# A third k pair in seven block products in the gate and up projections of a decoder trunk on one Trainium2 core

## The chip, the cores and the metric

The kernel runs on one core of a Trainium2 chip. The metric is the device time of one execution in microseconds, taken as the median of several runs. TensorE (PE) multiplies, VectorE (DVE) and ScalarE (ACT) prepare its operands, GpSimd (POOL) does little, and SyncE (SP) issues the weight loads.

## The reference: what is computed

Two decoder layers run over one sequence of 256 rows of width 2048, in float32. Layer 0 mixes by sliding-window attention and an mLSTM, layer 1 by forgetting attention. Every layer then has a SwiGLU feed-forward part of hidden width 5632, and a final RMS norm ends the trunk:

```python
def swiglu(xn, w_gate, w_up, w_down):
    return (jax.nn.silu(xn @ w_gate) * (xn @ w_up)) @ w_down
...
        h = h + mix.astype(h.dtype)
        h = h + swiglu(rms_norm(h, norm_ffn[layer]), w_gate[layer], w_up[layer], w_down[layer])
```

## The kernel before

**Three products for one.** Every large product is made of float32r operands. A tile is split into a rounded part `hi` (an ACT copy) and a rest `lo` (a DVE subtraction), and x·w becomes x_hi·w_hi + x_hi·w_lo + x_lo·w_hi: three matmuls of 128x128 against 128x512 (`three`, L344; `gemm`, L150). The activations are kept transposed and split in `xh`, `xl` (16 k tiles of 128, each with two row tiles t = 0, 1).

**Loads.** `load_raw` (L85) brings 256 rows of k by 512 columns (512 KB) on SP's queue into `raw`, which has four buffers. `split_chunk` (L138) makes `hi` and `lo` of it; these have four buffers each. So the raws of two k pairs are in the core at a time (one chunk of gate and one of up for each), and the splits of two.

**Gate and up.** `gate_up` (L352) makes one block of 512 hidden columns, for both row tiles, gate and up: four sums of 128x512. There are eleven blocks a layer, six and five with a down projection behind each group (`HALVES`), so 22 blocks in all. A block goes through eight k pairs in the order of this list, whose entries are (kind, pair):

```python
ORDER = ((0, 0), (0, 1), (1, 2), (0, 4), (0, 5), (1, 3), (0, 6), (0, 7))
MIXED = [p for w, p in ORDER if w]
```

A *plain* pair (kind 0, L359 to L370) splits one gate and one up chunk and makes 2 matrices x 2 k tiles x 2 row tiles x 3 = 24 matmuls into the four `plain` banks. A *mixed* pair (kind 1, L371 to L402) sees the same work as a 2x2 by 2x2 block product (rows: the two row tiles; inner: the two k tiles; columns: gate and up) and makes it of seven block products in place of eight, by sums of blocks: 7 x 3 = 21 matmuls. Four of the seven go into four banks of their own (`mixed`), three into `plain`. Its operands take more work: four differences of weight blocks (`t4`, L378 to L381), their splits `ht`, `lt` in two halves (L386 to L391, two buffers each; L240 and L241 within `split_plain`), the split of the gate chunk (L376), and that of half of the up chunk (L384). The sums of activations are made once a layer: `sums_of` (L199) fills one slot of `sh`, `sl` for each mixed pair, called from `split_scaled` (L213) while the output projection (`out_proj`, L332) delivers the layer's input, 512 columns (two k pairs) at a time.

**The end of a block.** The four mixed banks are folded into `c` (an ACT copy, L405, and four DVE additions, L406 to L409), then the four plain banks are added (L413), then come SiLU (L428), the product (L430), eight transposes (L438) and a split into the down projection's operands (L440 to L443).

**Banks.** PSUM has two pools of four banks. A block's plain banks lie in one pool and its mixed banks in the other, and the next block swaps them (`par`, L425). So the next block's plain sums start in the banks from which L405 to L409 have read, and its mixed products in those that L413 and the transposes have left.

**What sets the order.** The loops above give dependences and a priority; the framework's scheduler then fixes one order of instructions for each engine at build time, and PE's order interleaves neighbouring pairs and blocks. On the chip every engine goes through its own list in order and waits on semaphores.

Of the kernel before, what the change touches and what calls it, by code (L numbers as in the profile page):

```python
# [30 lines left out]
OFF_QM, OFF_KM, OFF_VM, OFF_OM = 1536, 2048, 2560, 3584  # L31
CAP = 15.0
FILL = 24
ORDER = ((0, 0), (0, 1), (1, 2), (0, 4), (0, 5), (1, 3), (0, 6), (0, 7))
MIXED = [p for w, p in ORDER if w]
HALVES = (0, 6, 11)

# [2 lines left out]
def trunk(  # L40
# [311 lines left out]
    def gate_up(fp, sh, sl, layer, g, par):  # L352
        c0 = g * NB
        plain = [[bank(par, "acc") for _ in range(NT)] for _ in range(2)]
        mixed = None
        count = [s_[0] for s_ in ORDER]
        for pos, (w, pair) in enumerate(ORDER):
            k0 = 2 * pair
            if not w:  # L359
                for m, wt in enumerate((w_gate[layer], w_up[layer])):  # L360
                    hi, lo = load_chunk(wt, k0, c0, NB)
                    for i in range(CK):
                        ah, al = x_of(k0 + i)
                        for t in range(NT):
                            ts = slice(t * P, (t + 1) * P)
                            three(
                                plain[m][t], ah[:, ts], al[:, ts], hi[:, i, :], lo[:, i, :],
                                pos == 0 and i == 0, pos == len(ORDER) - 1 and i == CK - 1,
                            )
# [518 lines left out]
```

## Time and profile before

| | |
|---|---|
| median of 3 runs | 2187.59 us (2187.58 to 2188.13) |
| the profiled execution | 2186.29 us, of it the profile's span 2184.6 us |
| granted TensorE clock, mean | 0.998 |
| busy: PE, DVE, ACT, POOL | 99%, 66%, 49%, 2% |
| HBM traffic | 186 GB/s over the span |
| matmuls of lines 345 to 347 (gate and up) | 3 x 1364 |

A row of the costliest groups gives busy time in total and the mean duration of one instruction; because an engine starts the next instruction before the last one is through, the spacing of starts in the timeline can be shorter than that duration. A timeline row gives the start in us, the duration in us, engine, line, operation, tiles, and in brackets the idle time before it with what ended it. Rows of SPq are the issues of loads.

In the text a pair is named by its kind and its place in the block's order: P0, P1, M2, P3, P4, M5, P6, P7 before. "Gate" and "up" are its two chunks.

### The profile page before, as it was taken

To read this page: it belongs to the slowest core of one execution; us is meant where nothing else is said; L and a number is where in the kernel's file an instruction comes from. 1 tells how busy PE (TensorE), PEld (TensorE's weight loads), DVE (VectorE), ACT (ScalarE), POOL (GpSimd) and SP (SyncE) were. 2 spreads that over 40 slices of the span, in tenths; PEclk is the share of its full clock that TensorE was granted. 3 is DMA by queue.
4 is the path that set the end of the run, shared out by engine and by line. 5 is a ranking of instruction groups with operands and counts; after the bars stand their busy time and mean duration, and the time that the engine had idled before them with its cause. 6 is when DMAs were issued, how large, how long until landed. Compare 5 with 4: busy or idle time off the path is not lost.

```text
span 2184.6 us, 26574 instructions
## 1 busy us (share of the span) xinstructions
PE 2164.8 (99%) x10052; PEld 1796.9 (82%) x10052; DVE 1442.0 (66%) x1732; ACT 1078.5 (49%) x1397; POOL 38.4 (2%) x61
## 2 busy tenths in 40 slices
PE   8999999999999999999999999999999999999998
PEld 6878888888888888888888888888888888888886
DVE  5565566788754677865555555668778645777754
ACT  5565455555543455544545544555455434554543
POOL 2110000000000000000010000000000000000000
PEclk9999999999999999999999999999999999999999
DMA  8544556666666666566675565566666665666664
GB/s 258 150 147 148 171 167 184 203 186 208 187 194 193 201 192 195 190 196 190 176 229 167 164 178 157 177 184 195 208 184 197 198 193 183 208 192 199 194 191 144
DMA packets 213536, 408.33 MB, mean 187 GB/s; under 512 B 12736, under 2 KB 21024, under 8 KB 213152
## 3 DMA queue, kind: packets, MB, share of 16 engines
q1 hardware_dynamic: 212736, 402.90, 60.0%
q0 software_dynamic: 624, 3.72, 0.5%
q8 instruction: 78, 1.28, 0.2%
q14 instruction: 50, 0.41, 0.1%
q10 hardware_dynamic: 48, 0.02, 0.0%
HBM read 404.48 MB, written 2.11 MB: 186 GB/s over the span
## 4 chain that ended last, share of the span: by engine, by line
PE 98%; ACT 1%; DMA 1%; issue 0%; DVE 0%; SPq 0%; POOLq 0%; POOL 0%; ACTq 0%
PE acc L164 17%; PE acc L165 17%; PE acc L166 17%; PE acc L346 12%; PE acc L347 12%; PE acc L345 12%; PE prod L346 2%; PE prod L345 2%; PE prod L347 2%; PE pf L438 1%; DMA h<-in_x_dram 1%; PE p L269 1%; PE ptm L252 1%; PE pt L219 1%; PE po L320 1%; PE pp L312 0%
## 5 line engine op out<-in xcount | busy, mean ns | idle before, releaser
L142 DVE TENSOR_TENSOR lo<-raw,hi 128x1024 fp32r<-128x1024 f32 (+3 forms) x732 | 876.7, 1206 | 597.0 <-ACT hi L141 595.7
L141 ACT CAST hi<-raw 128x1024 fp32r<-128x1024 f32 (+3 forms) x732 | 752.3, 1034 | 825.3 <-PE acc L166 515.1
L347 PE MATMUL acc<-hi,xl 128*128 128x512 f32 x1100 | 429.7, 391 | 0.0
L346 PE MATMUL acc<-lo,xh 128*128 128x512 f32 x1100 | 428.5, 390 | 0.0
L345 PE MATMUL acc<-hi,xh 128*128 128x512 f32 x1100 | 423.8, 391 | 0.0
L164 PE MATMUL acc<-hi,mh 128*128 128x512 f32 x768 | 300.6, 392 | 1.2 <-ACT mh L240 1.2
L165 PE MATMUL acc<-lo,mh 128*128 128x512 f32 x768 | 300.7, 392 | 0.0
L166 PE MATMUL acc<-hi,ml 128*128 128x512 f32 x768 | 298.3, 390 | 0.0
L165 PE MATMUL acc<-lo,xh 128*128 128x512 f32 (+3 forms) x736 | 276.3, 376 | 0.4 <-DVE lo L142 0.4
L164 PE MATMUL acc<-hi,xh 128*128 128x512 f32 (+3 forms) x736 | 275.2, 378 | 1.2 <-ACT hi L141 1.2
L166 PE MATMUL acc<-hi,xl 128*128 128x512 f32 (+3 forms) x736 | 276.2, 376 | 0.0
L347 PEld LDWEIGHTS acc<-hi,xl 128*128 128x128 f32 x1100 | 206.5, 188 | 42.5
L346 PEld LDWEIGHTS acc<-lo,xh 128*128 128x128 f32 x1100 | 206.6, 188 | 42.4
L345 PEld LDWEIGHTS acc<-hi,xh 128*128 128x128 f32 x1100 | 206.6, 188 | 41.9
L164 PEld LDWEIGHTS acc<-hi,mh 128*128 128x128 f32 x768 | 144.2, 188 | 31.0 <-ACT mh L240 1.4
L166 PEld LDWEIGHTS acc<-hi,ml 128*128 128x128 f32 x768 | 144.2, 188 | 29.7
L165 PEld LDWEIGHTS acc<-lo,mh 128*128 128x128 f32 x768 | 144.2, 188 | 29.4
L240 ACT CAST ht<-t 128x1024 fp32r<-128x1024 f32 x88 | 92.6, 1052 | 138.9 <-DVE t L379 113.6
L164 PEld LDWEIGHTS acc<-hi,xh 128*128 128x128 f32 x736 | 138.4, 189 | 26.5 <-issue 2.0
L165 PEld LDWEIGHTS acc<-lo,xh 128*128 128x128 f32 x736 | 139.1, 189 | 24.6 <-DVE lo L142 1.1
L166 PEld LDWEIGHTS acc<-hi,xl 128*128 128x128 f32 x736 | 139.1, 189 | 24.1 <-issue 0.3
L241 DVE TENSOR_TENSOR lt<-t,ht 128x1024 fp32r<-128x1024 f32 x88 | 107.2, 1218 | 0.0
(273 smaller groups left out, 1897.5 us busy)
## 6 DMA issues: line engine op xcount, KB each, us to landing
raw<-in_w_gate_dram SPq DMA_DIRECT2D x176, 512.0 KB, 4.0
raw<-in_w_up_dram SPq DMA_DIRECT2D x176, 512.0 KB, 4.5
raw<-in_w_down_dram SPq DMA_DIRECT2D x176, 512.0 KB, 3.7
raw<-in_w_in_odd_dram SPq DMA_DIRECT2D x88, 512.0 KB, 3.8
raw<-in_w_in_even_dram SPq DMA_DIRECT2D x64, 512.0 KB, 3.9
raw<-in_w_out_even_dram SPq DMA_DIRECT2D x32, 512.0 KB, 3.7
raw<-in_w_out_odd_dram SPq DMA_DIRECT2D x32, 512.0 KB, 3.7
raw<-in_w_in_odd_dram SPq DMA_DIRECT2D x8, 272.0 KB, 2.8
```

Source lines behind the costliest of these rows:

```text
L141: nc.scalar.copy(hi[:, :, 0:n], raw[:, :, 0:n])
L142: nc.vector.tensor_tensor(out=lo[:, :, 0:n], in0=raw[:, :, 0:n], in1=hi[:, :, 0:n].bitcast(F32), op=ALU.subtract)
L164: nc.tensor.matmul(o, ah[:, ts], hi, start=(k == 0), stop=False)
L165: nc.tensor.matmul(o, ah[:, ts], lo, start=False, stop=False)
L166: nc.tensor.matmul(o, al[:, ts], hi, start=False, stop=(k == k_all - 1))
L219: nc.tensor.transpose(pt[:, i, t, :], h[:, t, k * P : (k + 1) * P], ident)
L240: nc.scalar.copy(dst_h, src)
L241: nc.vector.tensor_tensor(out=dst_l, in0=src, in1=dst_h.bitcast(F32), op=ALU.subtract)
L252: nc.tensor.transpose(pt[:, i, :], s_, ident)
L345: nc.tensor.matmul(o, ah, hi, start=start, stop=False)
L346: nc.tensor.matmul(o, ah, lo, start=False, stop=False)
L347: nc.tensor.matmul(o, al, hi, start=False, stop=stop)
```

## The change

The order list gets a third mixed entry (pair 1), and the pairs are set out so that mixed ones stand at places 2, 4 and 6 with a plain one between:

```diff
-ORDER = ((0, 0), (0, 1), (1, 2), (0, 4), (0, 5), (1, 3), (0, 6), (0, 7))
+ORDER = ((0, 0), (0, 4), (1, 1), (0, 5), (1, 2), (0, 6), (1, 3), (0, 7))
 MIXED = [p for w, p in ORDER if w]
```

In the names above the order is then P0, P1, M2, P3, M4, P5, M6, P7. `sh` and `sl` grow by a slot (from 2 to 3), `sums_of` is called three times a layer in place of twice, and the place-1 pair of a block is k pair 4 where it was k pair 1. The number and size of the loads are the same.

## The prediction

> **What bounds the kernel now.** I read the page's busy times first, then what PE waits for, then one block of gate and up in the middle of the first group (449.87 to 493.00 us), as a window and instruction by instruction.
>
> ```profile
> PE 2164.8 (99%) x10052; PEld 1796.9 (82%) x10052; DVE 1442.0 (66%) x1732; ACT 1078.5 (49%) x1397; POOL 38.4 (2%) x61
> ```
>
> ```profile
> PE acc L164 <- ACT hi L141: 1.2, 2, 0.7
> PE acc L164 <- ACT mh L240: 1.2, 1, 1.2
> PE acc L165 <- DVE lo L142: 0.4, 2, 0.2
> ```
>
> Apart from the start, these are all the waits of PE that the view of waits lists (us, times, longest): none is at lines 345 to 347. In the blocks PE never waits. The window (busy us by engine, clock, DMA share, GB/s) says what room the others have:
>
> ```profile
> 449.87:493.00 43.13, 43.13 (x196) 35.69 (x195) 34.80 (x41) 22.25 (x25) 0.00 (x0) 1.00 0.64 195
> ```
>
> PE is busy all 43.13 us at clock 1.00, DVE 34.80, ACT 22.25. DVE is the next to bind, with 8.3 us to spare. PE's own pace is in its timeline, which runs through M5 (467.37 to 472.13) and P6 (to 477.57):
>
> ```profile
> 467.37 0.39 PE L345 MATMUL prod<-hi,xh 128*128 128x512 f32 x1
> ...
> 472.13 0.39 PE L345 MATMUL acc<-hi,xh 128*128 128x512 f32 x1
> ...
> 477.57 0.39 PE L345 MATMUL acc<-hi,xh 128*128 128x512 f32 x1
> ```
>
> 21 matmuls in 4.76 us and 24 in 5.44 are both 0.2267 us each. The 0.39 us of a row is latency, not pace: priced by it, a matmul would look 1.7 times too dear. A block is 186 matmuls (6 x 24 + 2 x 21), 42.16 us, and about 0.96 for its eight transposes.
>
> **What is removed.** One plain pair becomes mixed: 24 - 21 = 3 matmuls, 3 x 0.2267 = 0.68 us a block, 15.0 us over 22 blocks. A block would take 42.44 us. PE is the bound, so this is gained in full unless something else comes to be late.
>
> The Trainium skill (TensorE: Matmul & The Clock Gate, Back-to-back issue gap) gives 216 ns for an isolated gap at N=512 and a sustained 131 ns with weight loads between; the 66 matmuls would by these estimates be worth 14.3 or 8.6 us. The trace shows 0.2267 us with a weight load before each, so the measured pace decides.
>
> **What DVE gets.** Its timeline around M5's preparation, the folding of the mixed banks, and M2 of the next block:
>
> ```profile
> 458.42 0.69 DVE L378 TENSOR_TENSOR t<-raw 128x512 f32<-128x512 f32 x1 [1.66 <-issue]
> ...
> 460.96 1.22 DVE L241 TENSOR_TENSOR lt<-t,ht 128x1024 fp32r<-128x1024 f32 x1
> 462.10 1.22 DVE L142 TENSOR_TENSOR lo<-raw,hi 128x1024 fp32r<-128x1024 f32 x1
> 463.23 1.22 DVE L241 TENSOR_TENSOR lt<-t,ht 128x1024 fp32r<-128x1024 f32 x1
> 464.37 0.68 DVE L241 TENSOR_TENSOR lo<-raw,hi 128x512 fp32r<-128x512 f32 x1
> ...
> 472.68 0.69 DVE L406 TENSOR_TENSOR u<-prod,c 128x512 f32<-128x512 f32 x1
> ...
> 474.61 0.68 DVE L409 TENSOR_TENSOR c<-prod,c 128x512 f32<-128x512 f32 x1
> ...
> 483.90 0.69 DVE L378 TENSOR_TENSOR t<-raw 128x512 f32<-128x512 f32 x1 [0.50 <-DMA raw<-in_w_up_dram]
> ...
> 491.64 0.69 DVE L241 TENSOR_TENSOR lo<-raw,hi 128x512 fp32r<-128x512 f32 x1
> ```
>
> By starts, a mixed pair costs DVE 2.54 (four differences, 458.42 to 460.96) + 1.14 + 1.13 + 1.14 + 0.61 = 6.56 us; a plain one is two subtractions at 1.14, 2.28. The change adds 4.28 us a block: DVE goes from 34.80 to 39.1 of 42.44, 92%. ACT changes 2 x 1.05 for 1.05 + 0.62 + 2 x 1.05: 23.9 of 42.44. So both fit on average; the question is whether they fit in time.
>
> **Whether each preparation is in time.** I count from P0's first matmul (in the block before: 483.01 less the period of 43.12 is 439.9) and put PE's new places at 0, 5.4, then M2 at 11.8 (transposes before it), P3 16.5, M4 22.0, P5 26.7, M6 32.2, P7 36.9, next block 42.4. The raws have four buffers, so places 0, 2, 4, 6 share one half of them and 1, 3, 5, 7 the other. Now each half holds one mixed pair; then one half holds all three. A mixed pair keeps its raws from landing to the end of its preparation, so this half is a ring: release, load, prepare, release. From P0's release (480.08) to M2's first difference (483.90) is 3.8 us.
> M2 is as now: prepared among the last sums of the block before, its raws free at about 8.8 (now 491.64 - 483.01 + 0.61 = 9.2). M4's land at 13.0; DVE first does P3 and the split of the transposes, to 13.4; M4 then runs to about 20.0, its halves `ht` held back by M2's last use of that buffer at 16.5. PE wants M4's gate at 22.0, done 17.1, and `ht` at 24.0, done 18.3. M6's raws land at 24.2, P5 is split by then, and M6 is through at 30.8; PE wants its gate at 32.2 and the up half at 33.5. P0 of the next block lands at 35.0, is split by 37.1 for 42.4. M2's raws land at 41.2, before DVE is free for them at 42.1. So the ring closes inside the period, 0.9 us ahead of DVE, and every pair is 2 to 6 us ahead of PE. I take no stall.
>
> **What is late next.** The mixed banks: folding ends with L409 at 475.3, 7.7 us before the next block's first matmul at 483.01. M6 stands one place later, so 5.44 us of that go and 2.3 remain. If the cover is gone, each us late costs up to 22.
>
> **The once-a-layer edits.** A third `sums_of` is on ACT 2 x 0.46 + 0.59 and on DVE 4 x 0.29 + 0.69 us, for a pair of the first half of the output projection, with the whole second half's matmuls behind it; there (320 to 363 us) DVE is busy 28.96 of 43.00. In a layer's first block place 1 now needs columns 8 and 9 of k: their split ends at about 356.8, the block's first matmul is at 353.61, so place 1 is due at 359.0. I take 0 for both; bounds: nothing, or all of it bare, 3.4 us a layer, 6.7 in all. A gain is excluded, as nothing of PE's goes there. Loads are the same in number; 195 GB/s becomes about 198.
>
> **Sum.** 2186.29 (span 2184.6) - 15.0 = 2171.3 for the profiled execution. The median of the runs lies 1.3 above it, so 2172.6, with 2170 to 2177 as the case's own range: the few stalls of orders that fit less well cost 0 to 0.2 us a block.
>
> **Rivals.**
> *DVE becomes the bound (slower).* Place: each block's DVE queue. Its 39.1 us leave 3.3 a block. Against M's first difference DVE now waits on landings 46.2 us over 44 mixed pairs, 1.05 each; three make 3.2, so 42.3. That just fits, and it is the tightest number here. If successive instructions ran at their full durations, a block would be 19 x 1.22 + 25 x 0.69 + 2 x 0.74 = 41.9, with the waits 45.1. That is 2.7 over PE's period, 58 us, less the lead of about 3 us that each of four groups of blocks starts with: 2172.6 + 58 - 12 = 2219. It decides for slower from 43.12 + 0.5 = 43.7 us a block. For it: waits of up to 2.1 us at these differences. Against: starts 0.61 and 1.14 apart where the durations are 0.69 and 1.22, and that the first waiting of DVE now is for work that PE has not yet freed.
> The Trainium skill (VectorE: DVE Perf Modes, The TRN2 errata) gives a fp32 tensor_tensor (N+151)/0.96 ns: 691 and 1224 at N of 512 and 1024. The rows' durations agree; the starts show that part of it overlaps, so the rule taken as a pace speaks against this change more than the trace does.
> *The ring of raws is longer than I walk it (part of the gain).* With others' work in its midst M2's preparation now takes 483.90 to 492.25, 8.4 us. If all three do, the ring is 4 x 3.8 + 3 x 8.4 + 2.4 (P0's copy and subtraction) = 42.8: 0.4 over, 9 us: 2181. If P0 also keeps its buffers as long as now (9.8 us from issue 470.23 to 480.08, against 6.2), 46.4: 2172.6 + 4.0 x 22 - 12 = 2249.
> *The banks.* If DVE takes the next pairs' splits ahead of the folding and it ends 1 us after the banks are wanted, 22 us are lost: 2195. For it: one DVE queue at 92%. Against: the folding started 0.2 us after M5's last product.
> *It removes nothing:* I see no way; the matmuls are fewer whatever the order.
>
> **Chances.** Forecast 0.50; DVE bound 0.18; ring 2181 0.12, ring 2249 0.06; banks 0.06; between these and the forecast, the gain eaten up, 0.08. A measurement of this kernel can tell about 0.2%, 4.4 us: faster is below 2183.2, 0.62 (0.50 + 0.12); within 0.08; slower above 2192.0, 0.30 (0.18 + 0.06 + 0.06). The range 2169 to 2222 leaves out the ring's worst case, the upper half of the DVE case and a little below: some 0.17.
>
> **What the profile after would show.** Matmuls of lines 345 to 347: 3 x 1342 (now 3 x 1364). Transposes of one block 42.4 us from the next's. DVE busy 39 us in a block, and 1.0 us at most before each first difference. No wait of PE at lines 345 to 347. Wrong if PE waits there: for L241 or L142 speaks for DVE or the ring (told apart by whether DVE itself is idle, waiting on `raw`), for L405 to L409 for the banks. If DVE's busy share of a block is over 0.97, the first rival holds.

## The result and the profile after

The changed kernel takes 2190.8 us (17 runs) beside 2186.0 of the kernel before (17 runs): ratio 1.0021, 95% interval [1.0014, 1.0029]. It is slower by 0.2%, where 0.7% faster was forecast. The profiled execution is 2189.5 us, its span 2187.8 against 2184.6.

The page of the kernel after, busy times and the chain of work that ended last:

```profile
PE 2158.8 (99%) x9986; PEld 1782.2 (81%) x9986; DVE 1526.2 (70%) x1874; ACT 1118.1 (51%) x1447; POOL 37.6 (2%) x61
...
PE 65%; DVE 16%; DMA 13%; ACT 3%; issue 3%; SPq 0%; DVEq 0%; ACTq 0%; POOLq 0%; POOL 0%
```

The same line of the chain before:

```profile
PE 98%; ACT 1%; DMA 1%; issue 0%; DVE 0%; SPq 0%; POOLq 0%; POOL 0%; ACTq 0%
```

The 66 matmuls are gone (10052 to 9986). PE's busy share is still 99%, and by that nothing seems wrong; the chain says otherwise. Before it was 98% PE; now a third of it runs through loads, DVE and ACT. A matmul's row lasts 0.39 us while PE's pace is 0.2267 us, so two matmuls that start up to 0.39 us apart leave no gap in the busy share: inside the gate and up blocks the trace shows only 9.2 us of idle time on PE.

So the place has to be found by pace. This table counts, in the first group of the first layer, the time for every 186 matmuls of lines 345 to 347 (183 with three mixed pairs), from the timeline's starts (the sixth from its first start to its last, so one spacing less). The last three rows are kernels of the experiments:

| us for each block's matmuls | 1 | 2 | 3 | 4 | 5 | 6 |
|---|---|---|---|---|---|---|
| before | 43.15 | 43.13 | 43.13 | 43.13 | 43.13 | 42.90 |
| after | 42.47 | 42.87 | 43.20 | 45.20 | 44.63 | 44.13 |
| five raws | 42.46 | 42.41 | 42.45 | 42.97 | 42.41 | 43.26 |
| six raws | 43.15 | 42.42 | 42.43 | 42.41 | 42.43 | 42.87 |
| mixed at 2, 4, 5 | 42.47 | 42.41 | 42.41 | 42.43 | 42.44 | 42.21 |

The first block of the kernel after has the forecast's 42.4 us; then a lead is used up, and from the fourth on a block takes 44 to 45. Each down projection restores the lead: the shorter groups of five blocks only come to 43.7. All four groups together (first to last matmul) took 946.0 us and now take 949.9; with no stall they would take 931 (946.0 less the 15.0 of the matmuls). The 15 us were won and 19 lost again. Outside the groups nothing changed (1238.6 and 1237.8 us).

In the same block that the prediction looked at, the chain now reads (start, duration in us, what; the lines between are short steps):

```profile
454.58 4.58 DMA raw<-in_w_gate_dram
...
459.55 1.06 ACT hi L141
...
460.63 1.24 DVE lo L142
...
461.89 4.86 DMA raw<-in_w_up_dram
...
468.45 2.37 DVE lt L241 x2
...
473.91 5.14 DMA raw<-in_w_up_dram
...
481.46 4.62 DMA raw<-in_w_up_dram
...
486.20 0.69 DVE t L378
...
499.86 4.71 DMA raw<-in_w_gate_dram
```

PE is not on it. A load lands, is prepared, frees a raw buffer, and only then the next load can be issued: at 461.89, 0.02 us after the end of the subtraction that began at 460.63. Four such turns make one period, 499.86 - 454.58 = 45.3 us. The landings take 4.58 + 4.86 + 5.14 + 4.62 = 19.2 of it.

The waits on landings of gate and up, over the whole kernel (us, times, longest), show the same loop from the waiting engines. After:

```profile
ACT hi L141 <- DMA raw<-in_w_gate_dram: 81.5, 58, 3.7
...
DVE t L378 <- DMA raw<-in_w_up_dram: 52.3, 39, 2.9
...
ACT hi L240 <- DMA raw<-in_w_up_dram: 28.7, 26, 1.8
...
ACT hi L141 <- DMA raw<-in_w_up_dram: 16.8, 19, 1.7
```

Before:

```profile
ACT hi L141 <- issue: 48.5, 30, 3.1
DVE t L378 <- DMA raw<-in_w_up_dram: 27.2, 32, 2.0
ACT hi L240 <- issue: 26.4, 18, 1.6
DVE t L378 <- issue: 19.0, 12, 2.1
ACT hi L141 <- DMA raw<-in_w_up_dram: 3.5, 8, 0.9
```

ACT waits 127 us for landings, where before it waited under 4; DVE 52 where it was 27. The rows that end in "issue" name no releaser; the prediction counted DVE's 19.0 as waits on landings. With such rows counted on both sides (22.6 us of ACT's after), ACT goes from 78 to 150 us and DVE from 46 to 52. What such a wait costs is seen in what stands behind it. DVE's timeline at the end of that block:

```profile
482.69 0.68 DVE L406 TENSOR_TENSOR u<-prod,c 128x512 f32<-128x512 f32 x1
486.20 0.69 DVE L378 TENSOR_TENSOR t<-raw 128x512 f32<-128x512 f32 x1 [2.83 <-DMA raw<-in_w_up_dram]
...
487.42 0.68 DVE L407 TENSOR_TENSOR c<-prod,u 128x512 f32<-128x512 f32 x1
...
490.95 0.68 DVE L409 TENSOR_TENSOR c<-prod,c 128x512 f32<-128x512 f32 x1
```

DVE begins to fold the mixed banks, then stands 2.83 us before M2's first difference, whose raw has not landed, while the rest of the folding waits behind it. Its inputs are ready: in PE's timeline the last product into the mixed banks starts at 480.40 and its row lasts 0.39 us. The folding then ends in the midst of M2's preparation: 13.8 us from M2's landing at 486.08 to the next release on the chain at 499.84, that of P3's gate, which is split behind M2. ACT has the same thing with M6's up half ahead of M4's `ht`:

```profile
466.85 0.62 ACT L240 CAST hi<-raw 128x512 fp32r<-128x512 f32 x1 [1.60 <-DMA raw<-in_w_up_dram]
467.38 1.99 ACT L240 CAST ht<-t 128x1024 fp32r<-128x1024 f32 x2
```

What reaches PE in the end are short waits for late subtractions (weight loads of PE; us, times, longest):

```profile
PEld acc L346 <- DVE lo L142: 7.3, 7, 1.5
PEld acc L346 <- DVE lo L241: 7.3, 12, 0.7
```

DVE itself is busy 39.40 of 45 us in a late window (second figure: PE; fourth: DVE), so it has idle time; that speaks against the amount of its work as what holds the block up:

```profile
535.00:580.00 45.00, 43.20 (x191) 34.94 (x192) 39.40 (x48) 23.92 (x28) 0.00 (x0) 1.00 0.58 187
```

### The profile page after: what moved, and what is told of

Same layout as the page of the kernel before. It is cut to its first block, busy times and chain, and to the rows that moved or that the text cites. A ratio compares the mean times of both kernels' runs of the same rounds, so it can differ in the third digit from the quotient of the medians.

```text
span 2187.8 us, 26662 instructions
## 1 busy us (share of the span) xinstructions
PE 2158.8 (99%) x9986; PEld 1782.2 (81%) x9986; DVE 1526.2 (70%) x1874; ACT 1118.1 (51%) x1447; POOL 37.6 (2%) x61
## 4 chain that ended last, share of the span: by engine, by line
PE 65%; DVE 16%; DMA 13%; ACT 3%; issue 3%; SPq 0%; DVEq 0%; ACTq 0%; POOLq 0%; POOL 0%
PE acc L164 17%; PE acc L165 17%; PE acc L166 17%; DMA raw<-in_w_up_dram 9%; DVE lo L142 6%; DMA raw<-in_w_gate_dram 3%; PE acc L346 3%; PE acc L347 3%; PE acc L345 3%; DVE lt L241 2%; ACT hi L141 2%; DVE c L413 2%; DVE t L380 1%; DVE t L378 1%; PE prod L345 1%
## 5 line engine op out<-in xcount | busy, mean ns | idle before, releaser
L142 DVE TENSOR_TENSOR lo<-raw,hi 128x1024 fp32r<-128x1024 f32 (+3 forms) x710 | 851.2, 1202 | 490.2 <-ACT hi L141 488.1
L141 ACT CAST hi<-raw 128x1024 fp32r<-128x1024 f32 (+3 forms) x710 | 731.5, 1033 | 785.9 <-PE acc L166 498.0
L346 PE MATMUL acc<-lo,xh 128*128 128x512 f32 x946 | 369.9, 391 | 4.4 <-DVE lo L142 4.3
L347 PE MATMUL acc<-hi,xl 128*128 128x512 f32 x946 | 366.2, 390 | 0.0
L345 PE MATMUL acc<-hi,xh 128*128 128x512 f32 x946 | 349.8, 390 | 0.3 <-DVE c L407 0.3
L346 PEld LDWEIGHTS acc<-lo,xh 128*128 128x128 f32 x946 | 177.6, 188 | 43.5 <-DVE lo L142 7.3
L345 PEld LDWEIGHTS acc<-hi,xh 128*128 128x128 f32 x946 | 177.6, 188 | 38.3 <-DVE c L407 0.8
L347 PEld LDWEIGHTS acc<-hi,xl 128*128 128x128 f32 x946 | 177.7, 188 | 36.3
L240 ACT CAST ht<-t 128x1024 fp32r<-128x1024 f32 x132 | 137.3, 1052 | 120.9 <-DVE t L381 59.4
L241 DVE TENSOR_TENSOR lt<-t,ht 128x1024 fp32r<-128x1024 f32 x132 | 158.2, 1217 | 2.9 <-ACT ht L240 2.7
L164 PEld LDWEIGHTS acc<-hi,xh 128*128 128x128 f32 x736 | 138.3, 189 | 26.4 <-issue 2.0
L165 PEld LDWEIGHTS acc<-lo,xh 128*128 128x128 f32 x736 | 139.1, 189 | 24.7 <-DVE lo L142 1.1
L166 PEld LDWEIGHTS acc<-hi,xl 128*128 128x128 f32 x736 | 139.1, 189 | 23.9 <-issue 0.3
```

What stands on the lines that cost most here:

```text
L141: nc.scalar.copy(hi[:, :, 0:n], raw[:, :, 0:n])
L142: nc.vector.tensor_tensor(out=lo[:, :, 0:n], in0=raw[:, :, 0:n], in1=hi[:, :, 0:n].bitcast(F32), op=ALU.subtract)
L164: nc.tensor.matmul(o, ah[:, ts], hi, start=(k == 0), stop=False)
L165: nc.tensor.matmul(o, ah[:, ts], lo, start=False, stop=False)
L166: nc.tensor.matmul(o, al[:, ts], hi, start=False, stop=(k == k_all - 1))
L240: nc.scalar.copy(dst_h, src)
```

## The experiments

Two theories to tell apart. RING: the closed loop of raw buffer, load and preparation is longer than PE's block. DVE: VectorE's work, over 90% of a block, is the bound. Later a third question came up: what about the order makes the loop long.

**1. More raws.** Room for buffers is taken from the final norm's gains (and, for six, from a scratch tile):

```diff
-wr = tc.tile_pool(name="wr", bufs=4)
+wr = tc.tile_pool(name="wr", bufs=5)   # or 6
-    gf = cp.tile([P, D], F32, name="gf")
+        gf = sm.tile([P, NB], F32, tag="gf", name="gf", bufs=2)   # in finish; one buffer for six raws
```

> The changed kernel with a fifth buffer for raws; the room (4 KB) comes from the final norm's gains, loaded in two buffers of 512 columns in place of one tile of 2048. Theory RING (the three mixed pairs share two of four raw buffers, so release, load of 4.6 to 5 us, preparation, release closes in 44 to 45 us a block where PE needs 42.4): with five buffers the pairs no longer come back to the same two, and the ring has a fourth more room, so PE is the bound again: 2172 to 2178 us, blocks of 42.4 to 42.7. Theory DVE (VectorE at over 90% of a block is what PE waits for): nothing of its work goes, so 2186 to 2192, blocks of 44.

> The changed kernel with six raw buffers (room: the final gains in one buffer of 512 columns, one buffer less for squares nobody reads). Theory RING: three pairs' raws in turn, no waiting for loads at all, 2170 to 2174, blocks of 42.4 to the end of each group. Theory DVE (what is left after five buffers, blocks of 43 to 44.5 late in a group, is VectorE's): the same as with five, 2176 to 2180.

Five raws: 2177.7 us, ratio to the kernel before 0.9967 [0.9954, 0.9979]. Six raws: 2170.0 us, 0.9921 [0.9905, 0.9938]. Both theories could have lived with the first: its time is in RING's range, but late blocks still took up to 44.5 us (the last of the second layer's first group), where RING had said 42.7 at most. With six every block but a group's first and last is 42.4, and DVE has all its work in there. Windows of two blocks of the kernel with six raws:

```profile
449.00:491.40 42.40, 42.40 (x193) 35.11 (x192) 38.70 (x48) 23.44 (x27) 0.00 (x0) 1.00 0.66 210
491.40:533.80 42.40, 42.40 (x193) 35.13 (x192) 38.13 (x46) 23.96 (x28) 0.00 (x0) 1.00 0.61 196
```

PE is busy all 42.40 us with DVE at 38.7. The forecast's pace and its DVE sum were both right; only the loads were late. DVE's waits for landings at the first differences are still 38.6 us in all with six raws, so such a wait costs nothing where there are buffers enough.

**2. Is it the buffers themselves?** The same edits on the kernel before.

> The kernel before with the fifth raw buffer and the final gains in two small buffers: a control for what the room costs. PE is the bound in all its blocks, so both theories expect 2184 to 2188, the same as before.

> The kernel before with six raw buffers and the same savings of room: the control for six_raws. If the gain of six_raws is the third mixed pair's (RING, now with PE the bound at 42.4 a block), this one stays with the kernel before, 2183 to 2187, its blocks at 43.1. If the buffers themselves bring it, this one comes to 2172 to 2178 too.

2183.9 us, 0.9989 [0.9980, 0.9999], and 2183.6 us, 0.9989 [0.9979, 0.9998]. About 2 us of the 16 come with the buffers and the room made for them; blocks stay at 43.1. The rest is the third mixed pair's.

**3. DVE's load by itself.**

```diff
+        for _ in range(7):                      # dve_load_alone: once a block
...
+            nc.vector.tensor_tensor(out=junk, in0=h[:, 0, 0:NB], in1=h[:, 1, 0:NB], op=ALU.subtract)
...
+                    nc.vector.tensor_tensor(    # dve_load_spread: at each plain pair's gate chunk, and the first up chunk
+                        out=junk, in0=lo[:, 0, :].bitcast(F32), in1=lo[:, 1, :].bitcast(F32), op=ALU.subtract)
```

> The kernel before with seven more subtractions of 128x512 on VectorE in each block, of data that nobody uses (4.3 us a block, what the third mixed pair adds there), and no further mixed pair. Theory RING: the loads and the raw buffers are as before, so 2186 to 2189. Theory DVE: VectorE has as much to do as in the changed kernel while PE needs 43.1 us a block; PE waits, 2195 to 2215.

> The kernel before with seven more subtractions of 128x512 on VectorE in each block, of data that nobody uses, but now tied to their place: six read the rest of a plain pair's gate chunk just after it is made, the seventh that of the first up chunk (in the earlier run the scheduler had gathered all of them at the start of each group, so that run did not load the later blocks). VectorE then has 39 us of work in every block of 43.1, its share in the changed kernel. Theory RING: no load waits for another, PE stays the bound, blocks of 43.1, 2186 to 2190. Theory DVE: PE waits in the later blocks of a group, blocks of 44 and more, 2195 to 2215.

The first took 2195.3 us, 1.0045 [1.0030, 1.0059], which looked like DVE's theory. It was not the experiment meant: nothing tied the added work to its block, and the scheduler gathered it. In a layer's first group the first two blocks got 21 of the subtractions each, some 13 us; those of the second group ran in the down projection before it. The second block of each layer took 47.4 and 47.3 us, the first 43.5 and 43.1, and the rest were as before. In that 47.41 us block of the first layer DVE is busy 47.33 us, in the first block 42.63 of 43.46; so VectorE does hold PE up where it has more work than the block has time for, and hardly does at 98% of a block. The second run is the clean one: 2186.4 us, 0.9998 [0.9989, 1.0008], no loss. Its blocks, where DVE has what the change gives it:

```profile
493.00:536.10 43.10, 43.10 (x195) 35.69 (x194) 39.16 (x49) 22.61 (x26) 0.00 (x0) 1.00 0.61 196
536.10:579.20 43.10, 43.10 (x195) 35.68 (x195) 39.00 (x48) 22.46 (x26) 0.00 (x0) 1.00 0.63 195
```

DVE at 39 of 43.1 us (91%) does not slow PE when the loads have time, and with six raws 38.7 of 42.4 does not either. That takes the DVE theory down as a matter of quantity.

**4. Work taken off DVE.** The two products at a block's end (L430) go to ACT and GpSimd, with four raws and with five.

```diff
-                    nc.vector.scalar_tensor_tensor(out=c[:, t, :], in0=c[:, 2 + t, :], scalar=r[:, t : t + 1], in1=c[:, t, :], ...)
+                    nc.scalar.mul(c[:, 2 + t, :], c[:, 2 + t, :], r[:, t : t + 1])
+                    nc.gpsimd.tensor_tensor(out=c[:, t, :], in0=c[:, 2 + t, :], in1=c[:, t, :], op=ALU.mult)
```

> The changed kernel, four raws, with the two products at the end of a block (L430) taken off VectorE: ScalarE scales, GpSimd multiplies. VectorE loses 1.3 us a block. Theory RING: these products lie between the preparations of place 2 in one of four turns of the ring, so at most 1.3 us of a period is won: blocks 43.0 to 44.5, 2180 to 2191. Theory DVE: every block gets 1.3 us shorter as far as PE lets it: 2172 to 2178.

> Five raw buffers and the products off VectorE together. Theory RING: the same as five buffers alone, 2175 to 2179. Theory DVE for what is left: 2170 to 2174, blocks of 42.4 throughout.

2201.9 us, 1.0069 [1.0054, 1.0084], and 2192.0 us, 1.0027 [1.0017, 1.0037]: both missed, on the slow side, and neither theory had said so. What the first shows is a price of GpSimd (the last section): the products made DVE's other work longer by more than was taken off it, so as a test of DVE's share the two runs say little. Whether that price is all of the 11 us between the first and the changed kernel is not shown.

**5. Where the mixed pairs stand.** Only the list is changed, four raws; in the last one it is the list of the kernel before.

```diff
-ORDER = ((0, 0), (0, 4), (1, 1), (0, 5), (1, 2), (0, 6), (1, 3), (0, 7))
+ORDER = ((0, 0), (1, 1), (0, 4), (0, 5), (1, 2), (0, 6), (1, 3), (0, 7))   # mixed_at_1_4_6
+ORDER = ((0, 0), (0, 4), (1, 1), (0, 5), (1, 2), (1, 3), (0, 6), (0, 7))   # mixed_at_2_4_5
+ORDER = ((0, 0), (0, 4), (1, 1), (0, 5), (0, 6), (1, 2), (1, 3), (0, 7))   # mixed_at_2_5_6
+ORDER = ((0, 0), (0, 1), (1, 2), (0, 4), (1, 3), (0, 5), (0, 6), (0, 7))   # two_mixed_one_half
```

> The changed kernel with the mixed pairs at places 1, 4 and 6: one in one half of the raw buffers, two in the other; VectorE has the same work. Theory RING: each half has at most two preparations and two plain pairs a block, 2 x 7 + 2 x 2.4 + 4 x 4.8 = 38 us, below 42.4, so 2172 to 2180, unless the mixed banks, now wanted one pair after a block's start, hold it up. Theory DVE: 2186 to 2192.

> The kernel before, two mixed pairs, but at places 2 and 4, so that both share one half of the four raws, one plain pair apart as in the change. Theory RING, by the same sum: 39 us in the fuller half, below 43.1: no loss, 2184 to 2188. If spacing of one plain pair were itself the trouble, blocks of 43.5 and more, 2192 and up.

> The changed kernel, four raws, with the mixed pairs at places 2, 4 and 5: two in one half of the raw buffers, one in the other, at no room, the mixed banks free as early as before the change. Theory RING: the fuller half needs 4 x 4.8 + 8.4 + 6.6 + 2 x 2.4 = 39 us, so blocks of 42.4 to 43.0, 2172 to 2182, unless two mixed pairs side by side hold each other up at the two buffers of their split sums. Theory DVE has fallen; a rival is that any third mixed pair at four raws is too much: blocks of 44, 2186 to 2192.

> The changed kernel, four raws, with the middle mixed pair moved from place 4 to 5 and the last one kept at 6; with places 2, 4 and 5 it had no stall at all. Two readings of that: LAST PLACE (with the last mixed pair at 6 the folding of its banks falls into the preparation of the next block's place 2, which makes one turn from landing to release 13.8 us long): still slow here, blocks of 43.0 or more, 2178 to 2195. SPACING (mixed pairs one plain pair apart leave each load of a plain pair its full landing on the path; side by side they do not): fast here too, blocks of 42.4, 2169 to 2174.

| | us | ratio to the kernel before |
|---|---|---|
| mixed at 1, 4, 6 | 2183.9 | 0.9989 [0.9980, 0.9998] |
| two mixed, at 2 and 4 | 2186.2 | 1.0001 [0.9991, 1.0010] |
| mixed at 2, 4, 5 | 2170.9 | 0.9931 [0.9917, 0.9946] |
| mixed at 2, 5, 6 | 2189.0 | 1.0013 [1.0004, 1.0023] |

The third is the change with places 5 and 6 exchanged, and it has all of the forecast gain: the four groups take 930.7 us, each block at most 42.5. It came 1 us below its range. It settles the question of cause as far as the order goes. The spacing is not it: two mixed pairs one plain pair apart cost nothing, and two side by side are as slow as the change when the last stands at 6 and free of stalls when it stands at 5. With the last at 5 the folding has two plain pairs of cover, as before the change. DVE's timeline of that kernel, at a block's end:

```profile
516.80 0.68 DVE L406 TENSOR_TENSOR u<-prod,c 128x512 f32<-128x512 f32 x1
...
518.73 0.68 DVE L409 TENSOR_TENSOR c<-prod,c 128x512 f32<-128x512 f32 x1
...
524.30 0.69 DVE L378 TENSOR_TENSOR t<-raw 128x512 f32<-128x512 f32 x1 [0.23 <-DMA raw<-in_w_up_dram]
```

The folding goes through in one piece, 5 us ahead of M2's first difference, which finds its raw all but landed. The stretch that took 13.8 us after the change, from the landing of M2's up chunk to the issue of place 5's gate load, takes 9.7 us here (524.2 to 533.96). Leaving out each group's first block, it is 10.8 us in all blocks of the kernel before, 13.8 in 12 of 18 after the change (12.0 to 12.6 in the others), and 9.0 to 9.8 in 16 of 18 with places 2, 4 and 5. With places 2, 5 and 6 the loop is there again, and PE even waits for the banks themselves:

```profile
PEld acc L345 <- DVE u L406: 10.1, 8, 1.6
...
PEld acc L345 <- DVE c L409: 3.5, 9, 1.0
```

With places 2, 5 and 6 the mixed pairs are also spread over the two halves of the raws, if one counts by places as the prediction did, two and one, just as with 2, 4 and 5; so the halves do not decide either.

Places 1, 4 and 6 come out between, blocks of 42.5 to 43.6 apart from the groups' first; with the last at 6 too. Their 2183.9 us lies between the two theories' ranges and misses both: RING's had been summed by halves. What place 1 adds or saves there was not separated.

**The fastest versions** are the order 2, 4, 5 with four raws (2170.9 us) and the change with six raws (2170.0 us). The two aren't told apart: their intervals overlap. The first costs no memory.

## Why the prediction was wrong, point by point

- *What is removed.* Right. 3 matmuls a block at 0.2267 us: the stall-free kernel with places 2, 4, 5 is 15.3 us shorter in its four groups (946.0 to 930.7), forecast 15.0. The estimates from the gaps of the Trainium skill (TensorE: Matmul & The Clock Gate, Back-to-back issue gap), 14.3 and 8.6 us, came out lower than what was measured, the second by far.
- *What DVE gets.* Right in size: 39.1 us forecast, 38 to 39 measured. That it fits on average was true, and the spread load shows it by itself. The rule of the Trainium skill (VectorE: DVE Perf Modes, The TRN2 errata), taken as a pace, gave 41.9 us of work a block; the windows of six raws hold DVE busy 38.7 us in 42.4, so it holds for the duration of one instruction and not for the spacing of many.
- *Whether each preparation is in time.* This step failed, in three of its terms: the ring was walked round in 42.4 us with 0.9 us to spare, and the loop in the trace takes 45.3. The first term is the landing. The walk names 3.8 us a turn, read off a single turn, though its own steps are 4.1 to 4.2 (8.8 to 13.0, 20.0 to 24.2, 30.8 to 35.0, 37.1 to 41.2), 16.7 us in all. The four turns of the chain after average 4.8, 19.2 in all: 2.5 us more than walked, 4.0 more than four times 3.8. The profile before had the better number in its list of loads, a median of 4.5 us for up:

```profile
raw<-in_w_up_dram SPq DMA_DIRECT2D x176, 512.0 KB, 4.5
```

  The second is the folding: I put it before M2's preparation, and it runs within it, since the engine's list has M2's first difference ahead of the folding's second addition. From M2's landing to its release the walk had 10.0 us (41.2 to 8.8 in the next block); to the release that the loop waits for, 13.8 were measured. The third is the picture of two halves: by the times of issue a load takes whichever of the four buffers comes free (M6's up is issued at 461.89, as P5's gate leaves its buffer), so the loop ran through plain and mixed pairs alike. Its other three turns, from landing to release, took 2.7, 7.2 and 2.4 us, where the walk had 7.0, 6.6 and 2.1. So what lies between the landings came to 26.1 us, beside 25.7 in the walk: that this total is close is luck, as it is made of other parts.
- *What is late next.* The right place (the folding's cover, forecast to fall from 7.7 to 2.3 us), the wrong reason to fear it. It was priced as PE waiting for banks, which the kernel after shows once, for 0.8 us. What the timelines show in its place is the folding in the midst of the next block's first mixed preparation, and with it a longer loop of loads. (In the rival on the banks the folding starts 0.4 us after M5's last product, 471.90 + 0.39 to 472.68, and not 0.2; nothing hangs on it.)
- *The rivals.* The ring of raws was named, with a chance of 0.12 for 42.8 us a block and 0.06 for 46.4; 44 to 45 lies between the two, and my "gain eaten up" had 0.08. That a group starts with a lead was right, and it fits that the groups of five lose 1 to 3 us and those of six 7 to 8; its size, put at about 3 us, was not measured. The DVE rival, given 0.18, has fallen as a matter of quantity; of the 46.2 us of waits on landings in its sum, the view puts 19.0 down to no landing.
- *Once-a-layer edits* cost nothing that shows: outside the groups the time fell by 0.8 us.

What stays open: why the scheduler's list puts a difference ahead of a ready addition. That it reckoned with an earlier landing would fit, but no run here shows its reckoning. That the exchange of places 5 and 6 works through the folding, and not through some other shift of the order, is argued from four orders, their timelines and the length of the stretch behind M2's landing; the folding wasn't moved by itself.

## What to carry to other kernels

When an engine beside the one that binds comes to 90% and buffers are few, do not ask whether the work fits but how long the loop from a buffer's release to its next release is, with the landing times of the list of loads (median and worse), not the best turn in view. A change that moves the last user of a block closer to the block's end can take away the cover of what comes after it; look for what that work will collide with, on every engine that has it in its list. And try another order before more memory: here exchanging two entries brought what two more buffers brought.

## What the runs showed of the hardware that was not expected

GpSimd's products slow DVE down when both run. In the kernel with the products off DVE, the rows of the product and of the split sums (duration in ns, least, median, most):

```profile
L431 POOL TENSOR_TENSOR c<-c x44: 1292/2008/2285, 400.5 to 2084.4; 128x512 f32<-128x512 f32 x44
```

```profile
L241 DVE TENSOR_TENSOR lt<-t,ht x132: 1212/1222/2327, 359.4 to 2068.9; 128x1024 fp32r<-128x1024 f32 x132
```

In the kernel after, the same subtractions have

```profile
L241 DVE TENSOR_TENSOR lt<-t,ht x132: 1209/1217/1228, 358.6 to 2062.1; 128x1024 fp32r<-128x1024 f32 x132
```

1228 ns at most there and 2327 here; the one that began at 535.80 took 2.31 us while a product ran from 535.01 to 537.03. Over the whole trace, the two-input operations of DVE that overlap one of the 44 products are 42.5 us longer, all together, than the medians of their kinds. About 29 us (1.3 a block) had been taken off DVE, so its queue got more work, not less. The Trainium skill (SBUF — State Buffer, SBUF: two separate sides) says that a DVE operation with two SBUF inputs and a GpSimd operation that reads SBUF hold a shared port pair by exclusive lock, the other one blocked. By that rule the subtraction at 535.80 would wait for the product's end at 537.03, 1.2 us; it came out 1.1 us longer than the median, so the trace agrees.
